# A decoder block on one core: where the halves of the matmul operands lie in a partition

## The chip, the cores and the metric

The kernel runs on one core of a Trainium2 chip. The metric is the time of one execution on the device, in microseconds (us), lower is better. TensorE (PE in the profile) multiplies matrices, VectorE (DVE) and ScalarE (ACT) work elementwise, GpSimd (POOL) does a few small things, and SyncE's queue (SP) starts the transfers (DMA) between the large memory and the on-chip memory (SBUF). SBUF has 128 partitions; a tile takes the same bytes in each partition, so its place is one number, its first byte in a partition.

## What is computed

One decoder layer on 512 tokens of width 1024, in float32:

```python
h = rms_norm(x, g_mix_pre)
q, k, v, p_in, gm_u, gm_v, gate_in = split(h @ w_in)
merged = (sigmoid(gate0) * (stick_breaking_attention(q, k, v) @ w_br_sb)
          + sigmoid(gate1) * (multiscale_pool(p_in) @ w_br_pool)
          + sigmoid(gate2) * (chunked_spatial_gating(gm_u, gm_v) @ w_br_gm))
x = x + rms_norm(merged @ w_out, g_mix_post)
h = rms_norm(x, g_ff_pre)
x = x + rms_norm(square(relu(h @ w_ff_in)) @ w_ff_out, g_ff_post)
```

## The kernel before

Each float32 operand of a matmul is split in two tiles of a rounded 32-bit type: `hi` is the value rounded by ScalarE (`act.copy`), `lo` is what is left over, by VectorE (`tensor_sub`). A product is then three matmuls into one accumulator (`mm3`, lines 265 to 270): hi by hi, hi by lo, lo by hi. In each, the first-named operand is stationary (128 columns of it are loaded into the array by a weight load) and the other is moving (256 or 512 columns are streamed through it):

```python
(lh, ll), (rh, rl) = left, right
pe.matmul(ps, lhsT=lh, rhs=rh, ...)
pe.matmul(ps, lhsT=lh, rhs=rl, ...)
pe.matmul(ps, lhsT=ll, rhs=rh, ...)
```

Weights come in chunks of 1024 floats per partition. `load_chunk` (line 179) sends one or two transfers into a `raw` tile (3 buffers), `split_chunk` (line 188) turns it into a `whi` and a `wlo` tile (6 buffers each) and starts the next load. The normalised activations stand transposed in `hT0` (hi) and `hT1` (lo), made by `act_pair` (line 367). Work goes in this order: values of the attention (`psv`), the other projections and gates (`psc`, `psgv`), in between the attention in 16 units (`pt`, `z`, `av`), the branches (`psb`), the output projection (`acc`), then the channel mixer in four blocks. A block does eight projections (`psf` for the first four, `accf` after), whose squared relu is `ec`; `ff_act` (line 890) splits it and four sums of it into `ah` and `al`. Then seven products of half blocks (`accx`, `accy`, `accz`) take `ah`, `al` as stationary and `whi`, `wlo` as moving operand. In `psc`, `psb`, `psf` and `accf` it is the weights that are stationary, and `hT0`, `hT1` (or the branch's activations) move.

TensorE, ScalarE, VectorE and the SP queue run in the order in which the program is written, or nearly so (`InOrder`, line 80). GpSimd's instructions are placed by the scheduler.

Tiles are placed by pools that stand one after another in a partition: `cst` (constants), `wp` (`raw`, `whi`, `wlo`), `sm` (small), `ht` (`hT0`, `hT1`), `sb` (everything of the first part) and, over the same bytes later, `ff` (`ec`, `ah`, `al`, `t1`, `ys`). Three unused tiles, `space0`, `space1` and `space2` (`spacer`, line 57, each cleared once by GpSimd), lengthen the row so that `cst`, `wp`, `ht`, `sb` and `ff` each begin at a multiple of 512 bytes. Since `raw`, `whi`, `wlo`, `hT`, `ah`, `al` and the 2 KB slots of `sb` are multiples of 512 bytes long, each of these tiles begins at one too. Of the constants, `bsp`, `gmg`, `wph` and `wpl` begin 64 bytes past one.

Of the kernel before, what the change touches and what calls it, by code (L numbers as in the profile page):

```python
# [10 lines left out]
F32R = mybir.dt.float32r  # L11
# [6 lines left out]
P = 128  # L18
T = 512
D = 1024  # L20
NT = T // P
KD = D // P
# [26 lines left out]
def trunk_layer(ctx: ExitStack, tc: tile.TileContext, x, w_in, w_pool, pool_scale, gm_gain,  # L49
# [4 lines left out]
    o2 = out[0]  # L54


    def spacer(name, n):
        pool = ctx.enter_context(tc.tile_pool(name=name, bufs=1))
        nc.gpsimd.memset(pool.tile([P, n], F32, name=name), 0.0)

    spacer("space0", 96)
    cst = ctx.enter_context(tc.tile_pool(name="cst", bufs=1))
    spacer("space1", 24)
    wp = ctx.enter_context(tc.tile_pool(name="wp", bufs=1))
    sm = ctx.enter_context(tc.tile_pool(name="sm", bufs=4))
    spacer("space2", 32)
    ht = ctx.enter_context(tc.tile_pool(name="ht", bufs=1))
    dram = ctx.enter_context(tc.tile_pool(name="dram", bufs=1, space=bass.MemoryType.DRAM))

# [7 lines left out]
    def slot(ring, name, dt=F32):  # L77
        return home[0].tile([P, T], dt, name=name, tag=ring, bufs=RINGS[ring])
# [80 lines left out]
    FT = FF // P // NB  # L159
# [17 lines left out]
    loaded, made = [], []  # L177

    def load_chunk():
        raw = wp.tile([P, CHUNK], F32, name="raw", bufs=RAW)  # L180
        at = 0
        for v in plan[len(loaded)]:
            _, a, b = v.shape
            sp.dma_start(raw[:, at:at + a * b].rearrange("p (a b) -> p a b", a=a), v)
            at += a * b
        loaded.append(raw)

    def split_chunk(engines="v"):
        raw = loaded[len(made)]
        hi = wp.tile([P, CHUNK], F32R, name="whi", bufs=HL)  # L190
        lo = wp.tile([P, CHUNK], F32R, name="wlo", bufs=HL)
        if len(made) in derive:
            pieces = block_sums(raw, *derive[len(made)])
        else:
            pieces = [raw[:, n * CHUNK // len(engines):(n + 1) * CHUNK // len(engines)]
                      for n in range(len(engines))]
        at = 0
        for n, piece in enumerate(pieces):
            c = slice(at, at + piece.shape[1])
            at = c.stop  # L200
            e = engines[n % len(engines)]
            act.copy(hi[:, c], piece)
            (nc.gpsimd if e == "p" else dve).tensor_sub(lo[:, c], piece, hi[:, c].bitcast(F32))
        at = 0
        outs = []
        for v in plan[len(made)]:
            _, a, b = v.shape
            outs.append(tuple(t[:, at:at + a * b].rearrange("p (a b) -> p a b", a=a)
                              for t in (hi, lo)))
            at += a * b  # L210
        made.append(outs)
        if len(loaded) < len(plan):
            load_chunk()
# [3 lines left out]
    def block_sums(raw, stage, m):  # L217

        one, two = raw[:, :512], raw[:, 512:]
        if stage == "s1":  # L220
            t1s[m] = ff.tile([P, T], F32, name="t1", bufs=4)
            dve.tensor_add(t1s[m], one, two)
            return [one, t1s[m]]
        if stage == "s3":

            dve.tensor_add(t1s[m], t1s[m], one)
            dve.tensor_add(two, two, one)
            return [t1s[m], two]
        dve.tensor_add(two, two, t1s[m])
        return [raw]  # L230

    class Weights:
# [10 lines left out]
        def ready(self, i):  # L243
            live = self.chunks.start if self.keep else i
            while len(made) < min(len(plan), i + 1 + self.ahead, live + HL):
                split_chunk()
# [8 lines left out]
    def split(src, hi, lo, scale=None):  # L255

        if scale is None:
            act.copy(hi, src)
            dve.tensor_sub(lo, src, hi.bitcast(F32))
        else:  # L260
            act.activation(hi, src, AF.Copy, scale=scale)
            dve.scalar_tensor_tensor(lo, src, scale, hi.bitcast(F32), ALU.mult,
                                           ALU.subtract)
# [101 lines left out]
    act.activation(sm.tile([P, 1], F32, name="table"), zeros, AF.Sigmoid)  # L365

    def act_pair():
        return tuple(ht.tile([P, KD, T], F32R, name=f"hT{n}", tag=f"hT{n}", bufs=1)
                     for n in range(2))

    if True:
        hT = act_pair()

        def h_at(k, ts_=slice(0, T)):
# [29 lines left out]
        for step in V_ORDER.split():  # L404
            what = step.rstrip("0123")
            t, g = ([int(c) for c in step[len(what):]] + [0, 0])[:2]
            if what == "sq":
                if g == 0:
                    two[t] = sm.tile([P, 2], F32, name="n2")
                square_sum(xts[t][g], two[t][:, g:g + 1])  # L410
            elif what == "rms":
                rs[t] = rstd_d(two[t], "n")
            elif what == "scale":
                hns[t, g] = scaled(xts[t], rs[t], gpre, g)
            elif what == "turn":
                pts[t, g] = transposed(hns[t, g], bank("z", "trx"))
            elif what == "cols":
                split_to(hT, pts[t, g], t, g)
            elif what.startswith("split"):
                split_chunk(what[len("split"):])  # L420
            else:
                for which in {"hh": (0,), "rest": (1,), "mm": (0, 1)}[what]:
                    v_part(t, g, which)
# [201 lines left out]
        pool = [None] * 2  # L625
# [167 lines left out]
    def token_gemm(lhs, key, which, done, by_token, between=None, last=(WHOLE,)):  # L793
# [6 lines left out]
        for k0 in range(0, n, step):  # L800
            for t in range(NT):
                ts_ = slice(t * P, (t + 1) * P)
                for c in last if t == NT - 1 else (WHOLE,):
# [6 lines left out]
                    if k0 + step == n:  # L810
                        done(t, ps[t], c)

    h2 = act_pair()

    LAST = 1
# [40 lines left out]
    def between(t, k):  # L856

        if k == 2 and t >= 2:
            turn(t - 2)
        if k == 2 and t == 3:  # L860
            split_chunk("pp")
            later["ssq"] = residual(2, later["r"])
# [27 lines left out]
    def ff_act(f, ps):  # L890

        m, odd = divmod(f, 2)
        if not odd:
            pair_of[m] = ff.tile([P, 8, 256], F32, name="ec", bufs=2)
        ec = pair_of[m]
        rl = slot("tmp", "rl")
        act.activation(rl, ps, AF.Relu)
        act.activation(ec[:, 2 * odd:2 * odd + 2, :].rearrange("p a t -> p (a t)"), rl, AF.Square)
        if not odd:
            return  # L900
        a21, a11, a22, a12, q, n, s, r = (ec[:, i, :] for i in range(8))
        hi, lo = (ff.tile([P, 7, 256], F32R, name=x, bufs=FT // 2) for x in ("ah", "al"))
        split(ec[:, 1:4, :], hi[:, :3, :], lo[:, :3, :])
        dve.tensor_sub(q, a21, a22)
        dve.tensor_sub(n, q, a11)
        dve.tensor_sub(s, a11, a21)
        dve.tensor_add(r, n, a12)
        split(ec[:, 4:, :], hi[:, 3:, :], lo[:, 3:, :])
        parts[m] = hi, lo
# [11 lines left out]
    def block(which, p):  # L921
        return psum.tile([P, T], F32, name="acc" + which, tag=which, bufs=2)
# [26 lines left out]
    for b in range(NB):  # L949
        first = 0  # L950
        if b == 0:

            first = 4
            halves = slice(0, T // 2), slice(T // 2, T)
            wks = [Weights(("f1", b, f), ahead=2 - f) for f in (0, 2)]
            pss = [bank4("mm", f, "psf") for f in range(first)]
            for f in range(first):
                ff_in(pss[f], wks[f // 2], f % 2, halves[0])
                if f in (1, 2):
                    turn(f + 1)  # L960
            early.close()
            ff = ctx.enter_context(tc.tile_pool(name="ff", bufs=1, reuse_waits="tile"))
            home[0] = ff
            RINGS["tmp"] = 4
            gfpost = bcast_row(g_ff_post[0], [ff.tile([P, T], F32, name=f"gfpost{g}")
                                              for g in range(2)])
            Weights(("f1", b, first), ahead=2)[0]
            for f in range(first):
                ff_in(pss[f], wks[f // 2], f % 2, halves[1])
                ff_act(f, pss[f])  # L970
            act.on = dve.on = False
            banks.close()
            psum = ctx.enter_context(tc.tile_pool(name="psum2", bufs=1, space=PSUM,
                                                  reuse_waits="tile"))
            z = [block("z", p) for p in range(2)]
        for f in range(first, FT):
            if f % 2 == 0:
                wk = Weights(("f1", b, f))
            ps = block("f", f)
            ff_in(ps, wk, f % 2, slice(0, T))  # L980
            ff_act(f, ps)
        final = b == NB - 1
        if final:
            for i in range(2):
                pair = ff.tile([P, 2, D], F32, name="x1b", tag="ec", bufs=2)
# [21 lines left out]
        x = [block("x", p) for p in two]  # L1007
# [90 lines left out]
```

## Time and profile before

| | |
|---|---|
| median of 3 runs | 722.54 us (721.73 to 723.35) |
| the profiled execution, its own time | 722.87 us |
| its span, first to last instruction | 721.1 us |
| PE busy | 698.6 us (97%), 3320 matmuls |
| DVE busy | 494.0 us (68%) |
| ACT busy | 353.9 us (49%) |
| POOL busy | 54.0 us (7%) |
| chain that ended last | PE 80%, DVE 10%, DMA 4%, ACT 3%, issue 2%, POOL 1% |

The time is that of one whole execution; the span is what its instructions cover, 1.8 us less. The chain that ended last is followed back from the last instruction to whatever released it, step by step, so its shares say on what the end rested. A matmul's duration in this profile is longer than the time between two starts, since matmuls overlap; where many follow each other without a break, the chain's pieces give the time per matmul.

### The profile page before, as it was taken

How to read it: one execution, taken by the hardware profiler on the slowest of the kernel's cores; microseconds unless marked ns; L12 is line 12 of the kernel's file. 1: busy time of each engine (PE TensorE's matmuls, PEld its weight loads, DVE VectorE, ACT ScalarE, POOL GpSimd, SP SyncE). 2: the span in 40 equal slices, each digit the busy share in tenths (PEclk: the TensorE clock that was granted, in tenths of full speed). 3: DMA queues.
4: the chain of work that ended last, by engine and by line, in shares of the span. 5: the costliest groups of instructions: out<-in, count | busy, mean ns of one | idle time of the engine just before them, and what ended most of it. 6: DMA issues, size and time to landing. Idle time of an engine off the chain costs nothing.

```text
span 721.1 us, 9135 instructions
## 1 busy us (share of the span) xinstructions
PE 698.6 (97%) x3320; PEld 576.7 (80%) x3320; DVE 494.0 (68%) x771; ACT 353.9 (49%) x593; POOL 54.0 (7%) x106
## 2 busy tenths in 40 slices
PE   7999999999999999999999998999999999999994
PEld 4889887788888888888889777888888888888774
DVE  6745799777777544243576776747885679757897
ACT  6566666655444333321445654555534553445541
POOL 4100222111121000000040000000000000000001
PEclk9999999999999999999999999999999999999998
DMA  8272312322325233262325235633356234643543
GB/s 278 80 207 84 115 60 60 90 68 70 96 59 146 89 90 114 74 220 87 116 89 176 99 106 175 181 113 115 119 165 208 92 117 148 188 133 116 162 160 117
DMA packets 72432, 89.80 MB, mean 125 GB/s; under 512 B 4546, under 2 KB 49730, under 8 KB 72387
## 3 DMA queue, kind: packets, MB, share of 16 engines
q1 hardware_dynamic: 72384, 89.21, 39.5%
q8 instruction: 26, 0.43, 0.2%
q14 instruction: 20, 0.16, 0.1%
q10 hardware_dynamic: 2, 0.00, 0.0%
HBM read 85.01 MB, written 4.19 MB: 124 GB/s over the span
## 4 chain that ended last, share of the span: by engine, by line
PE 80%; DVE 10%; DMA 4%; ACT 3%; issue 2%; POOL 1%; SPq 0%; POOLq 0%; DVEq 0%; ACTq 0%
PE psc L90 25%; PE accf L90 18%; PE accx L90 7%; PE psb L90 6%; PE acc L90 6%; PE accz L90 5%; PE accy L90 4%; PE psv L90 3%; DMA raw<-in_w_ff_out_dram 3%; DVE wlo L90 2%; DVE ys L90 2%; PE psgv L90 2%; PE z L90 1%; PE av L90 1%; PE pt L90 1%
## 5 line engine op out<-in xcount | busy, mean ns | idle before, releaser
L90 DVE TENSOR_TENSOR wlo<-raw,whi 128x1024 fp32r<-128x1024 f32 (+1 forms) x145 | 158.1, 1095 | 109.6 <-ACT whi L90 108.8
L90 ACT CAST whi<-raw 128x1024 fp32r<-128x1024 f32 (+1 forms) x152 | 139.4, 927 | 140.5 <-PE psc L90 31.0
L90 PE MATMUL psc<-hT,whi 128*128 128x512 f32 x576 | 182.2, 398 | 0.0
L90 PE MATMUL accf<-hT,whi 128*128 128x512 f32 x448 | 138.1, 390 | 1.4 <-ACT rl L90 1.4
L90 PEld LDWEIGHTS psc<-hT,whi 128*128 128x128 f32 x576 | 103.9, 188 | 21.0 <-issue 1.5
L90 PE MATMUL psc<-hT,wlo 128*128 128x512 f32 x288 | 112.6, 391 | 0.0
L90 PEld LDWEIGHTS accf<-hT,whi 128*128 128x128 f32 x448 | 84.0, 188 | 19.1 <-ACT rl L90 1.8
L90 PE MATMUL accf<-hT,wlo 128*128 128x512 f32 x224 | 87.2, 389 | 0.0
L90 PEld LDWEIGHTS psc<-hT,wlo 128*128 128x128 f32 x288 | 54.1, 188 | 11.6
L90 PEld LDWEIGHTS accf<-hT,wlo 128*128 128x128 f32 x224 | 42.1, 188 | 8.8
L90 ACT CAST ah<-ec 128x768 fp32r<-128x768 f32 (+1 forms) x32 | 30.2, 944 | 32.6 <-DVE ec L90 32.1
L90 PE MATMUL accx<-whi,ah 128*128 128x512 f32 x96 | 37.9, 394 | 2.9 <-DVE ys L90 2.9
L284 POOL TENSOR_TENSOR pr<-pv,mhalf 128x1 f32<-128x1 f32 x8 | 4.8, 605 | 470.7 <-DVE pv L90 470.7
L90 DVE TENSOR_TENSOR al<-ec,ah 128x768 fp32r<-128x768 f32 (+1 forms) x32 | 34.8, 1087 | 4.7 <-ACT ah L90 4.5
L90 PE MATMUL accx<-wlo,ah 128*128 128x512 f32 x96 | 37.4, 390 | 0.0
L90 PE MATMUL accx<-whi,al 128*128 128x512 f32 x96 | 37.4, 390 | 0.0
L90 DVE TENSOR_TENSOR_SCAN nb<-nb,zeros 128x128 f32<-128x128 f32 (+3 forms) x32 | 27.5, 863 | 7.5 <-POOL nb L482 7.1
L90 DVE TENSOR_TENSOR ec<-ec 128x256 f32<-128x256 f32 x64 | 26.7, 421 | 7.0 <-ACT ec L90 6.7
L90 ACT CAST whi<-t 128x512 fp32r<-128x512 f32 x32 | 19.7, 616 | 14.8 <-DVE t L90 9.2
L90 PE MATMUL accy<-whi,al 128*128 128x512 f32 (+1 forms) x64 | 24.7, 386 | 1.9 <-DVE al L90 1.9
L90 ACT CAST a<-pt 128x128 fp32r<-128x128 f32 (+3 forms) x32 | 13.6, 426 | 25.9 <-PE pt L90 25.8
L90 ACT ACTIVATE sg<-psc 128x512 f32<-128x512 f32 x24 | 14.3, 598 | 22.7 <-PE psc L90 22.7
(197 smaller groups left out, 1236.0 us busy)
## 6 DMA issues: line engine op xcount, KB each, us to landing
raw<-in_w_ff_out_dram SPq DMA_DIRECT2D x96, 256.0 KB, 3.2
raw<-in_w_in_dram SPq DMA_DIRECT2D x42, 512.0 KB, 3.8
raw<-in_w_ff_in_dram SPq DMA_DIRECT2D x32, 512.0 KB, 3.9
xt<-in_x_dram SPq DMA_DIRECT2D x16, 256.0 KB, 6.3
raw<-in_w_out_dram SPq DMA_DIRECT2D x8, 512.0 KB, 3.7
raw<-in_w_ff_out_dram SPq DMA_DIRECT2D x8, 512.0 KB, 3.8
raw<-in_w_br_sb_dram SPq DMA_DIRECT2D x4, 512.0 KB, 3.4
x1d<-xt SPq DMA_DIRECT2D x8, 256.0 KB, 2.7
```

The lines of the kernel that those rows point to most:

```text
L90: i = op(*args, **kw).ins
L284: nc.gpsimd.tensor_tensor(r, v, mhalf, ALU.pow)
```

## The change

The three spacers are replaced by five others. Nothing is computed otherwise; the tiles' sizes and buffers stay. `space0` and `space1` go, `space2` grows, and new spacers lie between `whi` and `wlo`, between `hT0` and `hT1`, ahead of `ah`, and between `ah` and `al`.

```diff
-    def spacer(name, n):
-        pool = ctx.enter_context(tc.tile_pool(name=name, bufs=1))
+    def spacer(name, n, pool=None):
+        pool = pool or ctx.enter_context(tc.tile_pool(name=name, bufs=1))
         nc.gpsimd.memset(pool.tile([P, n], F32, name=name), 0.0)
 
-    spacer("space0", 96)
     cst = ctx.enter_context(tc.tile_pool(name="cst", bufs=1))
-    spacer("space1", 24)
     wp = ctx.enter_context(tc.tile_pool(name="wp", bufs=1))
     sm = ctx.enter_context(tc.tile_pool(name="sm", bufs=4))
-    spacer("space2", 32)
+    spacer("space2", 80)
     ht = ctx.enter_context(tc.tile_pool(name="ht", bufs=1))
...
         hi = wp.tile([P, CHUNK], F32R, name="whi", bufs=HL)
+        if not made:
+            spacer("space3", 16, wp)
         lo = wp.tile([P, CHUNK], F32R, name="wlo", bufs=HL)
...
     def act_pair():
-        return tuple(ht.tile([P, KD, T], F32R, name=f"hT{n}", tag=f"hT{n}", bufs=1)
-                     for n in range(2))
+        pair = []
+        for n in range(2):
+            pair.append(ht.tile([P, KD, T], F32R, name=f"hT{n}", tag=f"hT{n}", bufs=1))
+            if not n and not made:
+                spacer("space4", 64, ht)
+        return tuple(pair)
...
-        hi, lo = (ff.tile([P, 7, 256], F32R, name=x, bufs=FT // 2) for x in ("ah", "al"))
+        if not (b or m):
+            spacer("space5", 48, ff)
+        hi = ff.tile([P, 7, 256], F32R, name="ah", bufs=FT // 2)
+        if not (b or m):
+            spacer("space6", 80, ff)
+        lo = ff.tile([P, 7, 256], F32R, name="al", bufs=FT // 2)
```

The places in the two built programs, first byte in a partition and what is left of it by 512:

| tile | before | by 512 | after | by 512 |
|---|---|---|---|---|
| raw (first of 3) | 22016 | 0 | 21536 | 32 |
| whi (first of 6) | 34304 | 0 | 33824 | 32 |
| wlo (first of 6) | 58880 | 0 | 58464 | 96 |
| hT0 | 84992 | 0 | 84768 | 288 |
| hT1 | 101376 | 0 | 101408 | 32 |
| slots of sb (first) | 117760 | 0 | 117792 | 32 |
| ah (first of 4) | 146432 | 0 | 146656 | 224 |
| al (first of 4) | 175104 | 0 | 175648 | 32 |
| t1, ys (first) | 203776 | 0 | 204320 | 32 |

All instructions on TensorE, VectorE, ScalarE and the SP queue stand in the same order as before, with the same operands and the same waits. On GpSimd the clearing of spacers moves. At the program's start, before (space is a spacer, grow a row of gains for the first normalisation, ident the identity for transposes):

```order
L59 MEMSET space_58 128x96
L59 MEMSET space_66 128x24
L59 MEMSET space_77 128x32
L340 MEMSET grow 128x512
masks.py:197 MEMSET ident 128x128
L361 MEMSET mhalf 128x1
L363 MEMSET zeros 128x1
```

and now:

```order
L59 MEMSET space_67 128x80
L340 MEMSET grow 128x512
masks.py:197 MEMSET ident 128x128
L361 MEMSET mhalf 128x1
L363 MEMSET zeros 128x1
L59 MEMSET space_133 128x64
L59 MEMSET space_150 128x16
```

Two memsets have left the place ahead of grow, and two stand behind zeros. At the first block of the channel mixer, now (wlo is the lo half of a weight chunk, pr and nr are reciprocal roots for a normalisation; the names behind "waits" are semaphores, DMAHW those of transfers):

```order
L203 TENSOR_TENSOR wlo<-raw,whi 128x512 [waits DMAHW1_49,PE_49,Activation_49]
L284 TENSOR_TENSOR pr<-pv,mhalf 128x1 [waits DVE_49]
L284 TENSOR_TENSOR nr<-nv,mhalf 128x1 [waits DVE_49]
L59 MEMSET space_3808 128x48 [waits DMAHW6_49,DMAHW2_49]
L59 MEMSET space_3811 128x80
L284 TENSOR_TENSOR pr<-pv,mhalf 128x1 [waits DVE_49,Pool_49] x4
```

The two memsets are new; before, the last pr followed on nr directly.

## Rows read from the trace of the kernel before

**Rows 1.** Stages: us, then busy time (and count) of each engine, granted clock.
```profile
core 0: us, PE busy (x) PEld busy (x) DVE busy (x) ACT busy (x) POOL busy (x), PEclk, DMA share, GB/s
70.00:240.00 170.00, 169.42 (x833) 137.05 (x832) 136.65 (x243) 96.19 (x194) 31.88 (x66) 1.00 0.29 84
240.00:360.00 120.00, 120.00 (x531) 99.41 (x530) 51.81 (x64) 38.22 (x56) 1.10 (x2) 1.00 0.37 114
360.00:446.00 86.00, 79.67 (x452) 68.75 (x451) 63.28 (x101) 46.97 (x80) 7.97 (x9) 1.00 0.39 126
671.00:721.00 50.00, 39.41 (x183) 32.13 (x181) 41.03 (x73) 18.62 (x36) 2.16 (x4) 0.94 0.42 148
```

**Rows 2.** Chain that ended last: shares, then matmul pieces (start us, us, what).
```profile
PE 80%; DVE 10%; DMA 4%; ACT 3%; issue 2%; POOL 1%; SPq 0%; POOLq 0%; DVEq 0%; ACTq 0%
...
59.50 10.08 PE psgv L90 x84
282.88 21.76 PE psc L90 x96
464.39 43.52 PE accf L90 x192
```

**Rows 3.** Matmul groups by form, whole span: count, then busy us, mean ns.
```profile
L90 PE MATMUL psc<-hT,whi 128*128 128x512 f32 x576 | 182.2, 398 | 0.0
L90 PE MATMUL accf<-hT,whi 128*128 128x512 f32 x448 | 138.1, 390 | 1.4 <-ACT rl L90 1.4
L90 PE MATMUL psc<-hT,wlo 128*128 128x512 f32 x288 | 112.6, 391 | 0.0
L90 PE MATMUL accf<-hT,wlo 128*128 128x512 f32 x224 | 87.2, 389 | 0.0
L90 PE MATMUL accx<-whi,ah 128*128 128x512 f32 x96 | 37.9, 394 | 2.9 <-DVE ys L90 2.9
```

**Rows 4.** Timeline of TensorE: two matmuls with their weight loads.
```profile
141.13 0.40 PE L90 MATMUL psm<-pl,wph 128*128 128x512 f32 x1
141.13 0.19 PEld L90 LDWEIGHTS psm<-ph,wpl 128*128 128x128 f32 x1
```

**Rows 5.** The tile psm: duration ns min/median/max.
```profile
L90 PE MATMUL psm<-ph,wph x2: 479/490/502, 140.8 to 142.6; 128*128 128x512 f32 x2
...
L90 PE MATMUL psm<-pl,wph x2: 388/394/399, 141.1 to 142.9; 128*128 128x512 f32 x2
```

**Rows 6.** Matmul groups by form, 130 to 160 us.
```profile
L90 PE MATMUL psc<-hT,whi 128*128 128x512 f32 x58 | 18.7, 403 | 0.0
```

**Rows 7.** DVE groups by form: count, then busy us, mean ns.
```profile
L90 DVE TENSOR_TENSOR wlo<-raw,whi 128x1024 fp32r<-128x1024 f32 x108 | 131.4, 1222 | 96.3 <-ACT whi L90 95.8
...
L90 DVE TENSOR_TENSOR low<-av,low 64x256 f32<-64x256 f32 x16 | 6.6, 410 | 2.1 <-ACT low L90 2.1
...
L90 DVE TENSOR_TENSOR og<-pmix,bsp 64x256 f32<-64x256 f32 x8 | 3.4, 420 | 0.6 <-PE pmix L90 0.5
```

**Rows 8.** DMA issues: count, KB each, us to landing.
```profile
raw<-in_w_br_gm_dram SPq DMA_DIRECT2D x4, 256.0 KB, 3.2
...
bsp<-in_b_spatial_dram SPq DMA_DIRECT2D x4, 32.0 KB, 3.3
gmg<-in_gm_gain_dram SPq DMA_DIRECT2D x1, 128.0 KB, 3.1
wpb<-in_w_pool_dram SPq DMA_DIRECT2D x4, 16.0 KB, 2.2
```

**Rows 9.** Chain that ended last, its pieces of DMA.
```profile
1.71 5.72 DMA raw<-in_w_in_dram
...
669.95 4.85 DMA raw<-in_w_ff_out_dram
```

**Rows 10.** GpSimd: its spacers at the start, and its longest wait.
```profile
0.80 0.29 POOL L59 MEMSET space<- 128x96 f32 x3 [0.29 <-POOLq L1084]
...
POOL pr L284 <- DVE pv L90: 470.7, 6, 326.5
```

## The prediction

> **What bounds the kernel now.** I read the table of stages first, to see where TensorE is short of work, then the chain that ended last, for what a matmul costs where nothing interrupts it, then the groups by form, for how many matmuls there are of each kind, and at last the few rows in which an operand already lies off the 512-byte raster.
>
> TensorE is busy in all of 240 to 360 us, and in 169.42 of 170 us of the attention; 360 to 446 and the last 50 us leave it idle for 6.3 and 10.6 us [rows 1]. In the long unbroken pieces the price is constant: 96 matmuls of `psc` in 21.76 us, 192 of `accf` in 43.52, each 226.7 ns; the 256-column ones of `psgv` 10.08 us by 84, 120.0 ns [rows 2]. The clock granted there is full [rows 1], 2.4 GHz, at which 512 columns take 213.3 ns and 256 take 106.7. So each matmul costs its columns and a constant 13.3 ns, 32 periods of that clock. The change can gain or lose much only through this constant. At that price a matmul lasts 389 or 390 ns in the groups [rows 3].
>
> While one matmul streams, the next one's weights are loaded: the load of `wpl` stands at 141.13, the start of the matmul on `wph` [rows 4]. So TensorE reads two places of a partition at a time, and what the change moves is the distance of these two by 512 bytes. Before, it is 0 almost everywhere. After, in `psc`, `psf` and `accf` the load of `whi` (32) runs beside a stream of `hT0` (288): 256; the load of `wlo` (96) beside `hT1` (32): 64; then `whi` beside `hT0` again. In `accx`, `accy`, `accz` the load of `ah` (224) runs beside `whi` (32): 192; that of `al` (32) beside `wlo` (96): 448; and 192 again. These are the four distances.
>
> **The change part by part.**
>
> *TensorE.* The counts and order are unchanged. The groups concerned are 576+288 of `psc`, 448+224 of `accf`, 3 x 96 of `accx` [rows 3] (one of three rows stands there) and, in rows like it, 3 x 64 of `accz` and 3 x 60 of `accy`: 2196 matmuls; `psf`, `psv`, `psgv` and some of `acc` and `psb` come on top and are left out, since part of them lies in stretches with idle time. The trace of before has one place with another distance: the two matmuls on `pl` and `wph`, streaming from 0 while `wpl`, 64 past a multiple, is loaded. They last 388 and 399 ns [rows 5]. The steady 389 [rows 3] makes that -1 and +10 ns. But their neighbours at distance 0, in the same 30 us, last 403 on average where they take `whi` [rows 6] (the attention's short matmuls break the stream there, and the 403 holds matmuls that come first behind a break, as the `psm` ones of 479 and 502 ns do [rows 5]). So the value I take is 0: the two lie around what distance 0 gives nearby. The ends are -13.3 ns (the whole constant gone, as no row excludes) and +10 ns, for each of up to 2196. That the constant is the same 13.3 ns for 512 and 256 columns, and over `psc` and `accf`, whose tiles lie at quite different multiples of 512, speaks for a fixed cost of changing weights and against a collision.
>
> [...]
>
> *VectorE and ScalarE.* All big operands move from 0 to 32, 96, 224 or 288 past a multiple. The nearest rows: an addition with `bsp`, at 64, lasts 420 ns where one of the same 64x256 at 0 lasts 410 [rows 7], with PSUM as the other operand in both. The two differ in layout too (`bsp` is repeated), so I take 0; the ends are 0 and +10 ns in 410, 2.4%. VectorE carries 10% of the chain [rows 2], 72 us, so at worst 1.7 us reach the end. The rest lies beside TensorE's work: from 240 to 360 us VectorE is busy for 51.81 of 120 us [rows 1], and 2.4% of that, 1.2 us, would be the price there if TensorE were not the cover.
>
> *Transfers.* `raw` now begins 32 bytes past a multiple. Loads that already go to 64 past one: `gmg`, 128 KB in 3.1 us, beside 3.2 for 256 KB of `br_gm`, whose pieces are as long; `bsp`, 32 KB in 3.3 us, beside 2.2 for 16 KB of `wpb` [rows 8]. I take 0 by the first pair, where sizes are nearest to `raw`. The far end is the second pair's 1.1 us on each of the six loads that stand in the chain as pieces of their own (26.3 us in all; the first and the last are [rows 9], the others lie from 395 to 438 us): 6.6 us. Less than 0 I exclude: in no row does a load off the raster land sooner than one of its size on it.
>
> [...]
>
> *GpSimd.* Three memsets, 0.29 us together, stand ahead of `grow` [rows 10]; two go, two come behind `zeros`. At 0.1 us each either way nothing ends on them: the first weights arrive at 7.4 us [rows 9]. The two new ones in the mixer wait for transfers out of the bytes below, and behind them on GpSimd stands only the last `pr`, which waits 326.5 us for VectorE anyway [rows 10]. If that cover were gone they would cost some 0.25 us, from 0.1 us each and a wait.
>
> *Sum:* 0 on the profiled execution's 722.87 us. It stands 0.3 us above the median of 722.54; I forecast between them, **722.6 us**.
>
> **The rivals.**
>
> *The constant is a collision and goes.* For: all pairs lie at distance 0 before, and 32 periods is a suspiciously whole number. Against: the two matmuls at distance 64 did not fall under 388 ns [rows 5], and the same constant at 256 columns. 2196 x 13.3 = 29 us: **694**; if only the distance 256 frees it (two thirds of 1536 of `psc` and `accf`, 1024 x 13.3 = 13.6 us), 709.
>
> *New collisions.* The only row off the raster has one matmul 10 ns above the steady price [rows 5]; were it the distance and not the broken stream, then the distances 64 and 448, a third of 2196, 732 matmuls, would pay the mean of the two, 4.5 ns, 3.3 us in all: **726**; at 10 ns each 7.3 us, 730. It decides once a `wlo` load lengthens the matmul beside it in an unbroken stretch, where TensorE has no slack [rows 1]. This one ends slower.
>
> *Transfers off the raster are late*: up to **729.5** (722.9 and the 6.6 us above). Only waits at 395 to 440 and at 670 us, and the start, would feel it.
>
> *VectorE slower by up to 2.4%*: up to 724.6.
>
> **How the numbers follow.** A difference under 0.2% (1.45 us; the three runs of before spread by 1.62) can't be told from none. The forecast has 0.70: 0.62 within 0.2% and 0.04 each side, for scatter. The collision that goes has 0.10, all faster. New collisions have 0.09, all slower. Late transfers have 0.07, of which 0.05 over the bound; a slower VectorE 0.04, of which 0.03. So faster 0.04+0.10 = 0.14; slower 0.04+0.09+0.05+0.03 = 0.21; within 0.2% 0.62+0.02+0.01 = 0.65. The range runs from 719.5, below the forecast's scatter of about 3 us, to 727, which takes in the mild form of new collisions, VectorE's bound and most of late transfers; left out are the collision that goes (0.10) and the hard ends of the others (about 0.07).
>
> **What the profile after would show.** Right: pieces of 96 `psc` in 21.76 us and 192 `accf` in 43.52 us again, groups at 389 to 391 ns, the `wlo` split of 1024 at its old 1222 ns [rows 7], DMA pieces of the chain of the old lengths. Wrong: `accf` pieces near 41 us, or the groups of `whi` and `wlo` under one accumulator drifting apart (one distance costs and another does not), or longer DMA pieces at 395 to 440 us than the 3 to 5 us of before.

## The result, and the profile after

The changed kernel is slower: a median of 734.58 us over 4 runs (733.2 to 736.46) beside 722.94 us over 4 runs of the kernel before on the same chip (721.73 to 725.69). The ratio is 1.0157, with an interval of 1.012 to 1.0195. The forecast was 722.6 us, the range 719.5 to 727.0; the result lies outside it, on the side that had 0.21.

The profiled execution of the changed kernel took 736.46 us, the longest of its four, with a span of 734.8 us, 13.7 us more than the span of before. Most of it stands in the first line of the page:

```profile
PE 713.0 (97%) x3320; PEld 579.6 (79%) x3320; DVE 494.8 (67%) x771; ACT 354.1 (48%) x593; POOL 54.3 (7%) x108
```

TensorE is busy for 713.0 us where it was 698.6; its idle time fell from 22.5 to 21.8 us. VectorE and ScalarE changed by 0.8 and 0.2 us in all. So nothing new is waited for: the same 3320 matmuls take longer. Two stretches of the changed kernel, in the columns of [rows 1], the second its last 50 us:

```profile
240.00:360.00 120.00, 120.00 (x521) 97.38 (x520) 49.09 (x57) 36.39 (x50) 0.00 (x0) 1.00 0.34 105
684.80:734.80 50.00, 39.17 (x179) 31.52 (x177) 41.18 (x73) 18.08 (x36) 2.17 (x4) 0.95 0.41 143
```

In the 120 us in which TensorE has no pause it now gets 521 matmuls done, where it was 531, at the same granted clock of 1.00. The chain that ended last gives the price (start us, us, what):

```profile
PE 82%; DVE 7%; DMA 5%; ACT 2%; issue 2%; POOL 1%; SPq 0%; POOLq 0%; DVEq 0%; ACTq 0%
...
1.72 5.74 DMA raw<-in_w_in_dram
...
62.68 9.89 PE psgv L88 x84
...
248.56 5.55 PE psb L88 x24
...
287.39 22.19 PE psc L88 x96
...
331.76 35.49 PE acc L88 x153
...
472.98 44.36 PE accf L88 x192
...
534.13 11.20 PE accx L88 x48
...
682.87 4.50 DMA raw<-in_w_ff_out_dram
...
701.13 4.51 DMA raw<-in_w_ff_out_dram
```

Against [rows 2]: 96 of `psc` take 22.19 us instead of 21.76, 192 of `accf` 44.36 instead of 43.52. That is 231.1 ns a matmul instead of 226.7, or about 10 to 11 periods more. A period is here the time of one column: by [rows 2], 256 columns more take 106.7 ns more (226.7 against 120.0), 0.417 ns each, or 2.4 columns a ns; the forecast's 2.4 GHz shows here in this way alone. `psb` pays the same (5.55 us by 24 is 231 ns). `accx` stands at 11.20 us by 48, 233.3 ns. The 256-column matmuls of `psgv` became cheaper, 9.89 us by 84, 117.7 ns instead of 120.0.

The groups by form, which answer to [rows 3] and [rows 7], show where it sits, and where not:

```profile
L88 PE MATMUL psc<-hT,whi 128*128 128x512 f32 x576 | 183.0, 398 | 0.0
L88 PE MATMUL accf<-hT,whi 128*128 128x512 f32 x448 | 139.1, 391 | 1.2 <-ACT rl L88 1.2
L88 DVE TENSOR_TENSOR wlo<-raw,whi 128x1024 fp32r<-128x1024 f32 x108 | 131.5, 1223 | 98.5 <-ACT whi L88 98.1
L88 PE MATMUL psc<-hT,wlo 128*128 128x512 f32 x288 | 114.1, 396 | 0.0
L88 PE MATMUL accf<-hT,wlo 128*128 128x512 f32 x224 | 89.0, 397 | 0.0
L88 PE MATMUL accx<-whi,ah 128*128 128x512 f32 x96 | 38.6, 402 | 3.1 <-DVE ys L88 3.1
...
L88 DVE TENSOR_TENSOR og<-pmix,bsp 64x256 f32<-64x256 f32 x8 | 3.4, 421 | 0.6 <-PE pmix L88 0.5
```

Under one accumulator the two kinds have drifted apart, the sign the prediction gave for one distance that costs and another that does not: `accf` on `wlo` went from 389 to 397 ns, `accf` on `whi` from 390 to 391. Where every load is off, in `accx`, all are longer (394 before, 402 now). VectorE's split stands at 1223 ns, where it was 1222.

**The sum.** `psc` (864), `accf` (672) and `psb` (192 in the groups) are 1728 matmuls at 4.4 ns more, 7.6 us. The 192 of `acc` pay 5.3 ns (35.49 us by 153, where 34.68 stood, below), 1.0 us. The 660 of `accx`, `accz` and `accy` (288, 192, 180) go to 233.3 ns; their pieces before held 231.0 ns with small pauses in them (11.09 us by 48, below) and 226.7 without (all32, 10.88 us by 48 at 524.23 us), so 2.3 to 6.7 ns each, 1.5 to 4.4 us. The 96 of `psgv` and, if they behave alike, the 192 of `psf` give back 2.3 ns each, 0.7 us. Together 9.4 to 12.3 us, beside 11.6 us between the medians; `psv` and the attention's short matmuls are left out. The spans of the profiled pair differ by 2.1 us more than the medians do. Four pieces of the chain of before, which tell why, and what `acc` took:

```profile
35.87 21.76 PE psc L90 x96
...
326.40 34.68 PE acc L90 x153
...
605.99 11.09 PE accx L90 x48
...
700.60 5.53 PE accz L90 x24
```

and the first and the last of them in the changed kernel:

```profile
38.64 22.18 PE psc L88 x96
...
714.00 5.60 PE accz L88 x24
```

The `psc` piece starts 2.8 us later. Among all kernels run here this start lies anywhere from 34.95 to 38.64 us, without regard to their edits. From there to the `accz` piece the changed kernel loses 13.4 − 2.8 = 10.6 us, within the sum.

### The profile page after: what moved, and what is told of

The parts are those of the page before. It is cut to its first block, busy times and chain, and to the rows that moved or that the text cites. A ratio compares the mean times of both kernels' runs of the same rounds, so it can differ in the third digit from the quotient of the medians.

```text
span 734.8 us, 9138 instructions
## 1 busy us (share of the span) xinstructions
PE 713.0 (97%) x3320; PEld 579.6 (79%) x3320; DVE 494.8 (67%) x771; ACT 354.1 (48%) x593; POOL 54.3 (7%) x108
## 4 chain that ended last, share of the span: by engine, by line
PE 82%; DVE 7%; DMA 5%; ACT 2%; issue 2%; POOL 1%; SPq 0%; POOLq 0%; DVEq 0%; ACTq 0%
PE psc L88 26%; PE accf L88 18%; PE accx L88 7%; PE psb L88 6%; PE acc L88 6%; PE accz L88 5%; PE accy L88 4%; DMA raw<-in_w_ff_out_dram 4%; PE psv L88 3%; DVE wlo L88 2%; PE psgv L88 2%; PE z L88 1%; DVE ys L88 1%; PE pt L88 1%; PE av L88 1%
## 5 line engine op out<-in xcount | busy, mean ns | idle before, releaser
L88 PE MATMUL psc<-hT,wlo 128*128 128x512 f32 x288 | 114.1, 396 | 0.0
L88 PE MATMUL accf<-hT,wlo 128*128 128x512 f32 x224 | 89.0, 397 | 0.0
```

The lines of the kernel that those rows point to most:

```text
L88: i = op(*args, **kw).ins
```

## The experiments

Two theories stood against each other. **A tile's own place**: an operand that begins off a multiple of 512 (or of 64) bytes is read more slowly, or costs VectorE, ScalarE or a transfer more. **The distance**: what counts is how far the stationary operand lies from the moving one, by 512 or by 256 bytes. Each kernel below differs from the kernel before (or from the changed one, where that is said) by spacers or slices alone. Places are bytes in a partition.

**all32**: everything from `cst` on moves by 32 bytes, all distances stay 0.

```diff
-    spacer("space0", 96)
+    spacer("space0", 104)
```

> Before, with the first spacer 32 bytes longer, so that every tile stands 32 bytes past a multiple of 512 and all distances stay 0. Theory A (each tile's own place counts: 32 bytes off a multiple of 64 is slow): 192 accf in about 44.4 us as in the changed kernel, 84 psgv in 9.9 us, the time at 731 to 736 us. Theory D (the distance between load and stream counts): distances are 0, so 192 accf in 43.5 us and 722 to 724 us.

Measured: 722.07 us (10 runs) against 721.2 (13), ratio 1.001 (0.9989 to 1.003). Its chain:

```profile
60.82 10.08 PE psgv L90 x84
...
464.39 43.52 PE accf L90 x192
...
688.09 3.97 DMA raw<-in_w_ff_out_dram
```

The prices of before to the digit (120.0 and 226.7 ns). A tile's own place, 32 bytes off, costs nothing: not on TensorE, nor on VectorE (the split of 1024 at 1222 ns again), nor in the loads (`raw` from `w_in` lands in a median of 3.7 us, where before it was 3.8).

**dist64**: the changed kernel with a spacer of 96 bytes more ahead of `wp`. All the large tiles then lie at multiples of 64, at the same four distances.

```diff
     cst = ctx.enter_context(tc.tile_pool(name="cst", bufs=1))
+    spacer("space1", 24)
     wp = ctx.enter_context(tc.tile_pool(name="wp", bufs=1))
```

> The changed kernel with 96 bytes more ahead of the weights: the same four distances 256, 64, 192 and 448, but every tile at a multiple of 64 (128, 192, 384, 128, 320, 128 past one of 512). Theory A: as before, 192 accf in 43.5 us, 722 to 724 us. Theory D: as the changed kernel, 44.4 us and 733 to 737 us.

Measured: 730.5 us (4 runs) against 721.2, ratio 1.0131 (1.0108 to 1.0154). Its chain:

```profile
285.80 22.19 PE psc L89 x96
...
467.95 44.38 PE accf L89 x192
```

With the distances the price of the changed kernel is back, though none of the large tiles lies off 64. The whole stands below the 733 to 737 us expected; the ratio's interval overlaps that of the change. Together with all32 this ends the first theory.

**w32 and act32**: one distance for all. In w32 `whi` and `wlo` move by 32 and everything else stays; in act32 the weights stay and `hT`, the slots of `sb` and all of `ff` move by 32.

```diff
 w32:
-    spacer("space2", 32)
+    spacer("space2", 24)
...
+        if not made:
+            spacer("space3", 8, wp)
         hi = wp.tile([P, CHUNK], F32R, name="whi", bufs=HL)
 act32:
-    spacer("space2", 32)
+    spacer("space2", 40)
```

> Before, with whi and wlo alone 32 bytes past a multiple of 512; hT, ah, al, raw and all else at 0. In accf and psc the weights are stationary, in accx, accy, accz they move. Theory A: half of the cost or so; it shows in accf if the place of the stationary operand counts, in accx if that of the moving one does, 726 to 733 us. Theory D: distances 32 or 480 everywhere, slower in both groups, 730 us or more.

> Before, with everything behind the weights 32 bytes past a multiple of 512 (hT, ah, al, branches' operands), whi and wlo at 0: the counterpart of the run before. Theory A: accf (where hT moves) is slow if the moving operand's place counts, accx (where ah and al are stationary) if the stationary one's does; with the run before, the two costs should add up to that of all tiles at 32. Theory D: distances 480 or 32 in all groups, the same time as the run before.

Measured, against 721.2 us: w32 733.32 us, ratio 1.0164 (1.0143 to 1.0185); act32 732.96 us, ratio 1.0161 (1.014 to 1.0182). The chain of w32:

```profile
59.80 9.81 PE psgv L90 x84
...
285.62 22.40 PE psc L90 x96
...
468.84 44.79 PE accf L90 x192
```

and of act32:

```profile
468.80 44.80 PE accf L90 x192
```

Both come to 233.3 ns, 560 periods: the 512 columns and 48 periods, where before it was 32. Whether the weights or the activations are moved makes no difference, so it is the distance. 32 bytes are enough for 233.3 ns.

**w256 and w128**: w32 with `whi` and `wlo` 256 and 128 bytes off. They ask by what the distance counts.

```diff
 w256:
-    spacer("space2", 32)
+    spacer("space2", 96)
...
+            spacer("space3", 64, wp)
 w128:
-    spacer("space2", 32)
+    spacer("space2", 128)
...
+            spacer("space3", 32, wp)
```

> Before, with whi and wlo alone 256 bytes past a multiple of 512. Theory D256 (the distance counts by 256 bytes; the changed kernel's psc at 256, 64, 256 and psb at 0, 64, 0 cost the same): as before, 192 accf in 43.5 us, 721 to 723 us. Rival D512 (by 512 bytes, as the change is named): as with 32 bytes, 44.8 us, 732 to 734 us.

> Before, with whi and wlo alone 128 bytes past a multiple of 512. D256: slow as with 32 bytes, 192 accf in 44.8 us, 732 to 734 us. Rival D128 (by 128 bytes or less): 43.5 us, 721 to 723 us. 64 bytes cost in the changed kernel, so the raster isn't 64 or 32.

Measured, against 723.03 us (19 runs): w256 724.51 us (10 runs), ratio 1.0009 (0.9989 to 1.0029); w128 733.06 us, ratio 1.0135 (1.0113 to 1.0157). The chain of w256:

```profile
284.17 21.76 PE psc L90 x96
...
467.43 43.52 PE accf L90 x192
```

and of w128:

```profile
60.07 9.96 PE psgv L90 x84
...
468.53 44.61 PE accf L90 x192
...
552.17 44.79 PE accf L90 x192
```

256 is as good as 0 (724.51 us lies above the 721 to 723 expected, but the ratio's interval holds 1), and 128 is as dear as 32, or 0.9 ns a matmul less (44.79 and 44.61 us by 192 in two unbroken pieces). So the distance counts by 256 bytes, and the change's four distances by 512 (256, 64, 192, 448) are three by 256: 0, 64 and 192.

**no3**: the changed kernel without the spacer between `whi` and `wlo`, one part undone. `psc` and `accf` then have 256, 0, 256; in `accx` two loads of three stay at 192.

```diff
-    spacer("space2", 80)
+    spacer("space2", 96)
...
-        if not made:
-            spacer("space3", 16, wp)
```

> The change without the spacer between whi and wlo, all else at its changed place: psc, psf and accf at 256 only, psb and acc at 0, accx, accy, accz at 192, 0, 192. D256: 192 accf back at 43.5 us, the 48 accx still at 11.1 to 11.2 us, 725 to 727 us. D512: accf at 44.4 us or more, 731 us or more.

Measured: 724.63 us (10 runs) against 723.03 (19), ratio 1.002 (0.9997 to 1.0044). Its chain:

```profile
467.37 43.53 PE accf L88 x192
...
527.38 10.99 PE accx L88 x48
```

Without those 64 bytes nearly the whole loss is gone, though `raw`, `hT`, `ah`, `al` and all of `sb` stand where the change put them. The whole is just under the 725 to 727 us expected. `accx`, with two loads of three off, took 10.99 us by 48 in one piece and 11.11 in another that has a pause in it, where 11.1 to 11.2 had been forecast; 10.99 is 229.0 ns.

**wlo64**: the same part by itself, on the kernel before: `wlo` moved by 64 and nothing else. **w64**: `whi` and `wlo` both moved by 64, the same spacer one line higher, ahead of `whi`.

```diff
 wlo64:
-    spacer("space2", 32)
+    spacer("space2", 16)
...
         hi = wp.tile([P, CHUNK], F32R, name="whi", bufs=HL)
+        if not made:
+            spacer("space3", 16, wp)
         lo = wp.tile([P, CHUNK], F32R, name="wlo", bufs=HL)
```

> One part of the change alone: every tile as before, wlo alone 64 bytes further. In psc, psf, accf, psb and acc the distances by 256 are then 0, 64, 0, as in the changed kernel; in accx, accy, accz too (al is loaded while wlo streams). Theory that the distance by 256 sets the price and that one load of three off 0 costs two thirds of the full price: psc and accf at 231.1 ns (96 psc in 22.18 us, 192 accf in 44.37), accx between 230 and 233 (11.04 to 11.2 for 48), the whole 730 to 734 us. Rival that the loss of the changed kernel needs its other shifts too (hT1, sb, ah, al): psc and accf at or under 229 ns, the whole 723 to 728. Rival that each off load costs the same 6.6 ns as in w32: psc and accf 228.9 ns (96 in 21.97 us, 192 in 43.95), the whole near 728.

> As w32 and w128, with whi and wlo both 64 bytes off, so that every pair stands at 64. In the changed kernel one load of three stands at 64 and a triple is 13.2 ns longer; in w32 three of three stand at 32 and a triple is 19.8 ns longer. Theory that the price saturates at 48 periods whatever the distance: 233.3 ns each (96 psc in 22.40 us, 192 accf in 44.80), the whole 732 to 735. Rival that 64 is a dearer distance and its loads cost 13.2 ns each: 239.9 ns (23.03 and 46.06 us), the whole near 755 or more.

Measured, against 721.01 us (9 runs): wlo64 729.48 us (6 runs), ratio 1.01 (1.0067 to 1.0133); w64 730.26 us (4 runs), ratio 1.0116 (1.0064 to 1.0169). The chain of wlo64:

```profile
468.32 44.37 PE accf L90 x192
...
529.38 11.14 PE accx L90 x48
```

and of w64:

```profile
330.32 35.04 PE acc L90 x153
...
528.39 11.20 PE accx L90 x48
...
550.79 44.80 PE accf L90 x192
...
612.08 10.99 PE accx L90 x48
```

`wlo` moved by 64 alone gives the 231.1 ns of the changed kernel, and 729.48 us is just below the 730 to 734 expected. In `accf`, one load of three off costs two thirds of what three of three cost: a triple is 13.2 ns longer in wlo64 and 19.8 in w64. Since w64 stops at 233.3, 64 is not a dearer distance. Why one load takes two thirds was not found.

w64 as a whole missed its 732 to 735 us, for not all of its matmuls pay 233.3 ns. In `acc`, where the activations are stationary, 153 take 35.04 us, 229.0 ns; and of two pieces of 48 `accx`, with the same 64 bytes in the same execution, one takes 11.20 us (233.3 ns) and one 10.99 (229.0). So the distance says that a matmul costs more, but not alone how much.

**h16 and h4**: small distances, by slices of longer tiles. hT0 and hT1 stand 16 (or 4) bytes past a multiple of 256, all else as before.

```diff
-        return tuple(ht.tile([P, KD, T], F32R, name=f"hT{n}", tag=f"hT{n}", bufs=1)
-                     for n in range(2))
+        pair = []
+        for n in range(2):
+            t = ht.tile([P, KD * T + 64], F32R, name=f"hT{n}", tag=f"hT{n}", bufs=1)
+            pair.append(t[:, 4:4 + KD * T].rearrange("p (k t) -> p k t", k=KD))
+        return tuple(pair)
```

(h4 has `1:1 + KD * T` in place of `4:4 + KD * T`.)

> Before, with hT0 and hT1 alone 16 bytes past a multiple of 256, by a slice of a longer tile: psc and accf at 240 or 496, the mixer's second half and the branches at 0. D256 with no slack for small steps: 192 accf in 44.8 us, 48 accx in 10.9 us, about 1500 matmuls x 6.7 ns = 10 us more, 731 to 733 us. Rival (a distance inside one line of 32 bytes counts as 0): accf in 43.5 us, 721 to 723 us.

> As h16 with the halves of hT 4 bytes off (hT0 at 4, hT1 at 260 by 512), the rest as before. Theory that the price grows with the distance up to some point (16 gave 231.7 ns, 32 and more 233.3): psc and accf between 226.7 and 231.7 ns, say 228 (21.9 us for 96 psc, 43.8 for 192 accf), the whole 723 to 729. Rival that any distance but 0 or 256 costs the same: 231 to 233 ns (44.4 to 44.8 us for 192), the whole 729 to 733. Rival that a few bytes are enough to part two reads and nothing is paid: under 226.7 ns (192 accf under 43.5 us), the whole under 721.

Measured: h16 729.38 us (4 runs) against 723.03, ratio 1.0085 (1.0056 to 1.0113); h4 733.77 us (4 runs) against 721.01, ratio 1.0171 (1.0117 to 1.0224). The chain of h16:

```profile
467.26 44.48 PE accf L90 x192
```

and of h4:

```profile
248.98 5.46 PE psb L90 x24
...
470.19 45.69 PE accf L90 x192
...
532.24 10.88 PE accx L90 x48
```

16 bytes cost 231.7 ns, between the forecasts of full price and none, and 729.38 us lies between their ranges too. 4 bytes cost 238.0 ns, more than any larger distance, which none of the three expectations of h4 had. The matmuls that don't touch `hT` keep their price (`accx` 226.7 ns, `psb` 227.5). No other run moves an operand off a multiple of 32 bytes, so the price of the distance and that of the odd start can't be told apart here.

All of it side by side, in the 512-column matmuls of `accf` (piece of 192 divided by 192):

| kernel | distances by 256 in a triple | ns | ratio to before |
|---|---|---|---|
| before | 0 0 0 | 226.7 | |
| all32 | 0 0 0 | 226.7 | 1.001 |
| w256 | 0 0 0 | 226.7 | 1.0009 |
| no3 | 0 0 0 | 226.7 | 1.002 |
| the change | 0 64 0 | 231.1 | 1.0157 |
| dist64 | 0 64 0 | 231.1 | 1.0131 |
| wlo64 | 0 64 0 | 231.1 | 1.01 |
| h16 | 16 16 16 | 231.7 | 1.0085 |
| w128 | 128 128 128 | 232.3 to 233.3 | 1.0135 |
| w32, act32 | 32 32 32 | 233.3 | 1.0164, 1.0161 |
| w64 | 64 64 64 | 233.3 | 1.0116 |
| h4 | 4 4 4 | 238.0 | 1.0171 |

No version beat the kernel before. The 1.4 to 3.2 ns that a 256-column matmul gains off distance 0 would be under 1 us for 288 of them, and in every kernel that had it the 512-column ones lost far more.

## Why the prediction was wrong

*What bounds the kernel* was right: the price per matmul in unbroken stretches decides, the counts and waits stayed, and the change could only act through "a constant 13.3 ns", which the two prices of [rows 2] give by themselves: 2 x 120.0 − 226.7. The list of distances was right by 512; by 256, which counts, `psc` and `accf` have one pair of three off and `accx`, `accy`, `accz` all three.

*The step that failed* is TensorE's term: "So the value I take is 0". It measured 9.4 to 12.3 us. Two parts of its reasoning fell. The first is the reading of [rows 5]: of the two matmuls at distance 64, one stood 1 ns below and one 10 ns above the steady price, 4.5 ns on average, and I set that aside because neighbours at distance 0 averaged 403 ns in a broken stretch [rows 6]. A neighbour that is disturbed for another reason is no evidence that the row is undisturbed; the row stayed as open as it was, and its upper end should have had more than the 0.09. Nor were these two the only ones off: `wph`, like `wpl`, begins 64 bytes past a multiple, so every `psm` matmul was, and those on `wpl`, which follow the others without a break, stood at 395 against the steady 389, though in the same stretch:

```profile
L90 PE MATMUL psm<-ph,wpl x2: 392/395/398, 141.4 to 143.1; 128*128 128x512 f32 x2
```

The second is "speaks for a fixed cost of changing weights and against a collision". That 512 and 256 columns, and `psc` and `accf`, share a constant only showed that the constant does not depend on columns or on whole multiples of 512. All of them shared the distance 0 as well, so the rows of before could not say what it depends on. all32 and w256 confirm that multiples of 256 don't matter; w32 shows that the distance does.

*The rival "New collisions"* named the distance and the place, and its deciding sign, a triple that the `wlo` load lengthens in an unbroken stretch, came. But in the `accf` piece at 472.98 us the matmul beside which `wlo` is loaded lasts 392 ns where it was 389, and the `wlo` matmul itself 397, with the next start 236 ns behind its own where it was 226 or 227. Its size was off: 732 matmuls at 4.5 ns, 3.3 us, where 1728 in triples pay 4.4 ns on average, 192 of `acc` 5.3, and of the mixer's other 660 more than the third counted, because 192 and 448 are one distance by 256. By triples: an off load costs 13.2 ns and not 4.5, above the 10 ns taken as its upper end. The range to 727.0 took in only its mild form; with its end of 730 the range would still have missed.

*The rival that the constant goes* fell, for 512 columns in every run: 226.7 ns is the lowest price seen. The 13.3 ns stayed at every distance tried, and grew at most of them. Only the 256-column matmuls became cheaper, by 2.3 ns.

*VectorE and ScalarE*: 0 was right. The split went from 1222 to 1223 ns, `og` from 420 to 421 [rows 7].

*Transfers*: 0 was right as far as the sum above shows, which needs nothing from them. The first load in the chain took 5.74 us where it took 5.72, the one at 682.87 us 4.50 where 4.85 [rows 9]. The chain holds eight loads where it held six, among them one at 701.13 us; all32, which lost nothing, has such a late one too, at 688.09. The medians of landing are 0.1 to 0.4 us longer:

```profile
raw<-in_w_br_gm_dram SPq DMA_DIRECT2D x4, 256.0 KB, 3.4
...
bsp<-in_b_spatial_dram SPq DMA_DIRECT2D x4, 32.0 KB, 3.7
gmg<-in_gm_gain_dram SPq DMA_DIRECT2D x1, 128.0 KB, 3.4
wpb<-in_w_pool_dram SPq DMA_DIRECT2D x4, 16.0 KB, 2.5
```

beside 3.2, 3.3, 3.1 and 2.2 [rows 8]. In all32, with `raw` at 32 too, the same four landed in 3.2, 3.2, 3.1 and 2.3, so a start off the raster is not what moved them.

*GpSimd*: 0 was right. The spacers in the mixer stand where they should, and `pr` behind them waits for VectorE as before (its longest wait is 333.9 us, [rows 10]).

## What to carry to other kernels

Where TensorE bounds a kernel with a weight load beside every matmul, as here, the places of the two operands belong to its tuning: compare the stationary and the moving tile by 256 bytes in a partition, and keep that distance 0 for 512-column matmuls, which in `accf` took 226.7 ns at it and 231.1 to 238.0 off it. 32 bytes more in the spacer between two pools cost this kernel 1.6% (act32). When a forecast rests on a constant that every row shares, list what else all of them share; if the edit changes that, no row bounds it from inside, and a chance must go to a row off the raster even if it is one noisy pair.

## What the runs showed of the hardware that was not expected

- A 512-column matmul with a weight load beside it took 226.7 ns, 544 periods, when its stationary and moving operands lay a multiple of 256 bytes apart (before, all32, w256), and up to 233.3 ns, 560, when all three pairs of a triple lay 32, 64 or 128 bytes off (w32, act32, w64, w128): 32 periods over the columns, then up to 48. Some pieces paid less at the same distance, 232.3 ns in w128 and 229.0 in w64.
- Which of the pairs it is, the load and the stream that run at the same time or the two operands of one matmul, is not shown. In `psc`, `psb` and `accf` both give the same number of pairs off 0 in a triple. They part in `accx` of the changed kernel: load and stream lie at 192 all three times, a matmul's own operands at 192, 128 and 0. It pays 233.3 ns, and no3, with two of three off by either reckoning, 229.0. That leans to load and stream; that the `wlo` matmul of `accf` is the one that lasts longer (397 ns, where the one beside its load lasts 392) leans the other way; and w64 shows that one set of distances can have two prices.
- In `psgv`, with 256 columns, it goes the other way: 120.0 ns at distance 0, 116.8 (w32, 9.81 us by 84) and 118.3 (act32, 9.94 us) at 32, 117.7 at 64 (w64), 118.6 at 128 (w128).
- The parts of a triple don't add up, in `accf`: one load of three at 64 costs 13.2 ns (wlo64), three of three 19.8 (w64).
- The first guess about own alignment is wrong at 32 bytes: 32 past a multiple costs nothing by itself (all32, 226.7 ns). Under 32 bytes it may be different: a stream that begins 4 bytes past a multiple of 256 took 238.0 ns a matmul (h4), the highest price of all, one that begins 16 past 231.7 (h16).
- The two operands that TensorE reads are not without effect on each other: the same instructions with the same waits took 6.7 ns a matmul more when one of the two was moved by 32 bytes (w32 and act32, 233.3 ns), and none more when both were (all32, 226.7). By what mechanism, the runs don't show.
